# One set of transposes for the samples' x, rows by sequence, and state products on quarters of the array

## The chip, the cores and the metric

The kernel runs on one NeuronCore of a Trainium2 chip. Its engines are TensorE (matrix products; PE in the profile, its weight loads PEld), VectorE (DVE), ScalarE (ACT), GpSimd (POOL) and SyncE (SP), which here only issues transfers. Each engine works through its own list of instructions in order; semaphores make it wait for others. The metric is the device time of one execution in microseconds; the number given for a kernel is the median of its runs.

## What is computed

One step of a decoder layer with two branches, for one prompt of 256 tokens and 8 samples of 8 tokens each (320 tokens in all, D = 2048). The change lies in the second branch, a state-space scan with 32 heads of 64 in 4 groups, state size 128:

```
x = x + RMSNorm( W_out [ chunkMLP(h) || SSD(h) ] )        h = RMSNorm(x)
x = x + RMSNorm( ConvFFN(RMSNorm(x)) )

# SSD, per sequence and head:
h_t = exp(dt_t a) h_{t-1} + dt_t x_t B_t^T        y_t = h_t C_t
# so the state after a sample's 8 tokens is
#   exp(sum of dt a) * state + sum over its tokens of (decay to the end * dt * x_t) B_t^T
```

Each of the 8 samples brings a state of its own (per group 128 x 512: state size by 8 heads of 64), which is read from memory, used, updated and written back.

## The kernel before, in words

**Layout.** Activations stand transposed, 128 features on the partitions and 320 tokens along the row: 256 of the prompt, then 64 of the samples. Products with the big weights run in split float32: each operand is a rounded part (hi) and a remainder (lo), and `accumulate` (lines 151 to 155) makes three products hi*hi, lo*hi, hi*lo of 128 x 128 weights by 320 columns. These are the "ordinary products" of the text. A "slab" is 512 KB of weights: SyncE loads it (`slab`, line 118), ScalarE rounds it (whi, line 124), VectorE subtracts (wlo, line 125); each of raw, hi and lo has three buffers, and a slab feeds some 24 ordinary products.

**Order of the work.** The order of the instructions on every engine is fixed when the program is built, by a planner: it takes instructions by priority, which is their order in the program unless a block is marked as more urgent, and reckons with durations of its own for when an operand will be there. Small work runs in the background: generators (`steps`, `layer_norm`, `gate_mix`, `ssd`, `norm`) are advanced by one step with every `tick` (line 165), one or more ticks behind each slab, so that their instructions stand between ordinary products. The stage of the four `ssd` groups runs from about 430 to 755 us of the trace, beside the last input projections and the products with W_out; its last state update stands at 827 us.

**Time steps (`steps`, 467 to 552).** dt, its softplus, and the sums of dt a are made for five blocks of token rows: two of the prompt, one of the samples, and two in which 32 sample tokens stand fourfold on the 128 partitions (line 473). The decays to the end of a sample come from a mask `later_s`, made by GpSimd in two parts (line 544), each followed by a small TensorE product (line 546) into dec_ps. L773 and L774 are GpSimd copies of the next stage that wait for the same memory as dacsT (the transfer at line 531) to come free.

**B by tokens (775 to 786).** B is transposed by TensorE (`by_token`, line 393; tile bt_ps) for the prompt's two blocks and for the samples' two halves of four samples, the latter copied fourfold first (`fourfold`, line 397). Of the four quarters of partitions two keep the rounded part and two the remainder: bsp.

**One group (`ssd`, 799).** `x_of_samples(i)`, called for each half i = 0, 1, copies x fourfold (x4, line 397), transposes it (four products xt_ps, line 393), multiplies by dt times the decay (xq, line 824), rounds (xsp, line 841), subtracts (line 842), and puts the samples' part of xdt beside it (two products of line 824). The group's states are then taken in four pairs i = 0..3, one of each half of the samples:

- `with_c(i)` (yo_ps, line 887): C times the old states, on TensorE at four column positions of 32.
- `picked(i)` (bm, line 892): ScalarE copies bsp with every row outside the samples of this pair multiplied by zero (bsel).
- `shrunk(i)` (line 898): GpSimd multiplies the old states by their decay.
- `grown(i)` (up_ps, line 904): for either half one TensorE product bm x xsp over all 128 rows, which thus adds the three products hi*hi, hi*lo, lo*hi and a fourth, lo*lo; VectorE adds it to the state (line 906).
- `store_state(i)` (line 911): ScalarE's queue writes the two states back; the fourth pair's are loaded into the memory of the first (lines 805 to 810, six buffers).

The steps are spaced by `yield`: x_of_samples(0); begin(0); a step in which x_of_samples(1) stands; begin(1) and end(0); an empty step; begin(2) and end(1), and so on (lines 932 to 948). `begin` is with_c, picked and shrunk; `end` is grown and store_state. In the last group end(3) is put off behind the last product with W_out (lines 1017 and 1088).

Behind the state updates come the decays within a chunk (`decays`, 956 to 973: ScalarE exponentials cs and cpx, fed by the transfer at line 816) and the products for y (`products`, line 983: y_ps, TensorE at two column positions of 64).

## Time and profile before

| | |
|---|---|
| median of 3 runs | 1779.02 us (1778.82 to 1779.88) |
| profiled execution | 1781.37 us, of which the traced span is 1779.7 us |
| granted TensorE clock, mean over the span | 0.999 |
| VectorE busy | 1168.0 us |
| ScalarE busy | 819.5 us |
| GpSimd busy | 273.5 us |
| moved by transfers | 289.91 MB, 163 GB/s on average |

The profile is that of one execution. A row of a timeline gives start, duration, engine, line and operation, out<-in, partitions x elements and type, and how many such instructions were merged (x8); in brackets the idle time ahead of it and what ended it. For a TensorE product the name of the moving operand comes first, then that of the weights, and "128*32" says rows x columns of the weights. Products are pipelined, so the distance from one start to the next tells more than the duration. The chain is the path of work that ended last, followed back from the end; its rows give start, time on the chain, engine, tile and line. A waits row gives who waited for whom: total us, how many times, the longest.

### The profile page before, as it was taken

To read this page: it belongs to the slowest core of one execution; us is meant where nothing else is said; L and a number is where in the kernel's file an instruction comes from. 1 tells how busy PE (TensorE), PEld (TensorE's weight loads), DVE (VectorE), ACT (ScalarE), POOL (GpSimd) and SP (SyncE) were. 2 spreads that over 40 slices of the span, in tenths; PEclk is the share of its full clock that TensorE was granted. 3 is DMA by queue.
4 is the path that set the end of the run, shared out by engine and by line. 5 is a ranking of instruction groups with operands and counts; after the bars stand their busy time and mean duration, and the time that the engine had idled before them with its cause. 6 is when DMAs were issued, how large, how long until landed. Compare 5 with 4: busy or idle time off the path is not lost.

```text
span 1779.7 us, 30655 instructions
## 1 busy us (share of the span) xinstructions
PE 1770.5 (99%) x11933; PEld 1715.7 (96%) x11933; DVE 1168.0 (66%) x1999; ACT 819.5 (46%) x1195; POOL 273.5 (15%) x602
## 2 busy tenths in 40 slices
PE   9999999999999999999999999999999999999998
PEld 7789999999999998999999999999999999999998
DVE  7549764656977768677865464756656575656575
ACT  5434555334564547445545333343434343433445
POOL 1202200000331313103121011110102020101004
PEclk9999999999999999999999999999999999999999
DMA  7546645456665665554554545545545545454543
GB/s 260 163 148 177 189 128 154 153 153 188 216 190 190 181 207 168 168 171 145 180 156 146 157 149 151 155 148 152 157 144 156 150 150 155 150 150 155 147 154 107
DMA packets 214417, 289.91 MB, mean 163 GB/s; under 512 B 16384, under 2 KB 143744, under 8 KB 214080
## 3 DMA queue, kind: packets, MB, share of 16 engines
q1 hardware_dynamic: 202544, 268.74, 49.6%
q10 hardware_dynamic: 10016, 14.16, 2.2%
q0 software_dynamic: 1712, 5.05, 1.0%
q8 instruction: 94, 1.54, 0.4%
q14 instruction: 51, 0.42, 0.1%
HBM read 273.08 MB, written 14.82 MB: 162 GB/s over the span
## 4 chain that ended last, share of the span: by engine, by line
PE 97%; DVE 1%; ACT 0%; DMA 0%; issue 0%; POOL 0%; POOLq 0%; ACTq 0%; DVEq 0%
PE ps L153 19%; PE ps L155 19%; PE ps L154 19%; PE pd L153 10%; PE pd L155 10%; PE pd L154 10%; PE ps_v L144 7%; PE y_ps L983 1%; PE up_ps L904 0%; PE yo_ps L887 0%; PE sg L731 0%; PE xt_ps L393 0%; DMA cs<-dacs_d 0%; PE x1p L1278 0%; PE tsum L296 0%
## 5 line engine op out<-in xcount | busy, mean ns | idle before, releaser
L125 DVE TENSOR_TENSOR wlo<-wraw,whi 128x1024 fp32r<-128x1024 f32 (+1 forms) x476 | 582.5, 1224 | 432.4 <-ACT whi L124 430.1
L124 ACT CAST whi<-wraw 128x1024 fp32r<-128x1024 f32 (+1 forms) x475 | 494.8, 1042 | 729.9 <-PE ps L154 392.1
L153 PE MATMUL ps<-h_hi,whi 128*128 128x320 f32 x2268 | 704.0, 311 | 0.0
L154 PE MATMUL ps<-h_lo,whi 128*128 128x320 f32 x2268 | 702.7, 310 | 0.0
L155 PE MATMUL ps<-h_hi,wlo 128*128 128x320 f32 x2268 | 702.2, 310 | 0.0
L153 PEld LDWEIGHTS ps<-h_hi,whi 128*128 128x128 f32 x2268 | 426.2, 188 | 2.6 <-issue 1.6
L154 PEld LDWEIGHTS ps<-h_lo,whi 128*128 128x128 f32 x2268 | 426.3, 188 | 0.7
L155 PEld LDWEIGHTS ps<-h_hi,wlo 128*128 128x128 f32 x2268 | 426.2, 188 | 0.0
L155 PE MATMUL pd<-fhi,wlo 128*128 128x320 f32 x704 | 218.2, 310 | 0.0
L153 PE MATMUL pd<-fhi,whi 128*128 128x320 f32 x704 | 218.2, 310 | 0.0
L154 PE MATMUL pd<-flo,whi 128*128 128x320 f32 x704 | 218.2, 310 | 0.0
L153 PE MATMUL pd<-ohi,whi 128*128 128x320 f32 x448 | 139.4, 311 | 0.0
L155 PE MATMUL pd<-ohi,wlo 128*128 128x320 f32 x448 | 138.7, 310 | 0.0
L154 PE MATMUL pd<-olo,whi 128*128 128x320 f32 x448 | 138.7, 310 | 0.0
L153 PEld LDWEIGHTS pd<-fhi,whi 128*128 128x128 f32 x704 | 132.1, 188 | 0.0
L154 PEld LDWEIGHTS pd<-flo,whi 128*128 128x128 f32 x704 | 132.1, 188 | 0.0
L155 PEld LDWEIGHTS pd<-fhi,wlo 128*128 128x128 f32 x704 | 132.1, 188 | 0.0
L1180 POOL COPY ptf<-pad 128x2 f32<-128x2 f32 x88 | 21.0, 239 | 603.7 <-DVE pad L1168 603.0
L249 DVE TENSOR_TENSOR acc_ffn<-acc_ffn,pd 128x320 f32<-128x320 f32 (+1 forms) x161 | 77.5, 482 | 37.8 <-PE pd L155 36.5
L153 PEld LDWEIGHTS pd<-ohi,whi 128*128 128x128 f32 x448 | 84.1, 188 | 1.4 <-issue 1.0
L154 PEld LDWEIGHTS pd<-olo,whi 128*128 128x128 f32 x448 | 84.1, 188 | 0.3
L155 PEld LDWEIGHTS pd<-ohi,wlo 128*128 128x128 f32 x448 | 84.1, 188 | 0.1
(328 smaller groups left out, 1867.9 us busy)
## 6 DMA issues: line engine op xcount, KB each, us to landing
wraw<-in_ffn_w_up SPq DMA_DIRECT2D x176, 512.0 KB, 3.7
wraw<-in_w_in SPq DMA_DIRECT2D x140, 512.0 KB, 3.8
wraw<-in_ffn_w_down SPq DMA_DIRECT2D x88, 512.0 KB, 3.4
wraw<-in_w_out SPq DMA_DIRECT2D x64, 512.0 KB, 3.4
st<-in_state_ssm SPq DMA_DIRECT2D x32, 256.0 KB, 3.9
out_ssm_state_sample<-st ACTq DMA_DIRECT2D x30, 256.0 KB, 3.4
cs<-dacs_d SPq DMA_DIRECT2D x16, 320.0 KB, 4.7
xr<-in_xT SPq DMA_DIRECT2D x4, 640.0 KB, 4.0
```

The costliest lines, as they stand in the source:

```text
L124: rounded[:] = [act.copy(hi, raw).ins]
L125: dve.tensor_tensor(out=lo, in0=raw, in1=hi.bitcast(F32), op=ALU.subtract)
L144: made = pe.matmul(out, xi, w[g][wi], start=first and begins, stop=last and ends)
L153: pe.matmul(ps, whi, xhi, start=first, stop=False)
L154: pe.matmul(ps, whi, xlo, start=False, stop=False)
L155: return pe.matmul(ps, wlo, xhi, start=False, stop=last).ins
L249: added_last[:] = [dve.tensor_tensor(out=acc[:, nb, ts], in0=acc[:, nb, ts], in1=ps[:, ts], op=ALU.add).ins]
L983: pe.matmul(ps[64 * i:64 * i + 64, cols], w(hl), x(hl, m, cpx), tile_position=(0, 64 * i), **flags)
L1180: pool.tensor_copy(ptf[:, k, :], pad[:, 256:258])
```

## The change

- x and B of the samples are transposed once, 64 tokens on 64 partitions, not twice on four copies of 32 tokens. The fourfold copies, the second `x_of_samples` and the masked copies of B (`picked`, bsel) go.
- The rounded part and the remainder are made on these 64 partitions, and then moved by transfers on ScalarE's queue (`by_sequence`) into rows ordered by sequence: partition 4t + c holds part c of the t-th token of a half, so that the 32 rows of one sequence (8 tokens, four parts) are one quarter of the partitions. Eight transfers of 32 rows x 512 elements (64 KB) for B, and eight for x in every group.
- `grown` multiplies 32 rows only, at the row position of the quarter of its sequence (`tile_position=(q, 0)`). The two products of a pair come from different quarters (`of_half`), go to two PSUM tiles and are issued one behind the other, ahead of both additions; the pairs are now samples i of the first half and (i + 1) % 4 of the second.
- `steps` works on three blocks of token rows instead of five: three dt products, one mask `later_s` of 64 x 64, made one step earlier (ahead of csT_ps), and one product with it.

The steps between begin and end, all other loads, stores and products, and the last group's postponed end(3) keep their places. The diff:

```diff
-            for i in range(2):
-                pool.tensor_copy(dtf[:, (3 + i) * P:(4 + i) * P].rearrange("p (q t) -> p q t", q=4),
-                                 dtf[:, NP + 32 * i:NP + 32 * i + 32].unsqueeze(1).to_broadcast([P, 4, 32]))
             yield
             ps = misc("dt_ps")
-            for c in range(5):
+            for c in range(3):
                 pe.matmul(ps[:, NH * c:NH * c + NH], dtf[:, P * c:P * c + P], sums[:, 0], start=True, stop=True)
...
+            later_s = tp.tile([P, NT], F32, tag="pv", name="later_s", bufs=4)[:NS, :NS]
+            pool.tensor_tensor(out=later_s, in0=later[:NS, :NS], in1=bd, op=ALU.mult)
             ps = misc("csT_ps")
             for c in range(2):
                 pe.matmul(ps[:NH, P * c:P * c + P], da[:, c], upper, start=True, stop=True)
...
             pe.matmul(ps[:, 2 * NH:3 * NH], ones, da[:, 1], start=True, stop=True)
-            later_s = tp.tile([P, NT], F32, tag="pv", name="later_s", bufs=4)[:NS, :2 * P].rearrange("p (r q t) -> p r q t", r=2, q=4)
-            for r in range(2):
-                rs = slice(32 * r, 32 * r + 32)
-                pool.tensor_tensor(out=later_s[:, r], in0=later[:NS, rs].unsqueeze(1).to_broadcast([NS, 4, 32]),
-                                   in1=bd[:, rs].unsqueeze(1).to_broadcast([NS, 4, 32]), op=ALU.mult)
-                pe.matmul(ps[:, (3 + r) * NH:(4 + r) * NH], later_s[:, r].rearrange("p q t -> p (q t)"), da[:NS, 2],
-                          start=True, stop=True)
-            act.activation(dec.rearrange("p c h -> p (c h)"), ps[:, :H5], AF.Exp)
-            dve.tensor_tensor(out=dt[:, 3:5], in0=dt[:, 3:5], in1=dec[:, 3:5], op=ALU.mult)
+            pe.matmul(ps[:NS, 3 * NH:4 * NH], later_s, da[:NS, 2], start=True, stop=True)
+            act.activation(dec[:, :3].rearrange("p c h -> p (c h)"), ps[:, :3 * NH], AF.Exp)
+            act.activation(dec[:NS, 3], ps[:NS, 3 * NH:4 * NH], AF.Exp)
+            dve.tensor_tensor(out=dt[:NS, 3], in0=dt[:NS, 2], in1=dec[:NS, 3], op=ALU.mult)
...
             pool.tensor_copy(cb[NS:, NT:], ident[NS:, NS:])
-            for c in range(4):
+            def by_sequence(out, which, parts):
+                rows = out.rearrange("(t c) i n -> t c i n", c=4)
+                for i in range(2):
+                    for c, w in enumerate(which):
+                        act.dma_start(rows[:, c, i].bitcast(F32), parts[w].bitcast(F32)[32 * i:32 * i + 32])
+            for c in range(3):
                 ps = misc("bt_ps")
-                b4 = bT if c < 2 else fourfold(sd.tile([P, 4, P], F32, tag="xde", name="b4", bufs=2), bT, c - 2)
+                n = NS if c == 2 else P
                 for g in range(4):
-                    by_token(ps[:, P * g:P * g + P], b4[:, g], c if c < 2 else 0)
+                    pe.transpose(ps[:n, P * g:P * g + P], bT[:, g, P * c:P * c + n], ident)
                 if c < 2:
                     act.copy(btok[:, c, :], ps)
                 else:
-                    b = bsp[:, c - 2]
-                    act.copy(b, ps)
-                    for rs in (slice(32, 64), slice(96, P)):
-                        dve.tensor_tensor(out=b[rs], in0=ps[rs], in1=b[rs].bitcast(F32), op=ALU.subtract)
+                    parts = [sd.tile([NS, 512], F32R, tag=t, name="part", bufs=n) for t, n in (("bm", 1), ("xde", 2))]
+                    act.copy(parts[0], ps[:NS])
+                    dve.tensor_tensor(out=parts[1], in0=ps[:NS], in1=parts[0].bitcast(F32), op=ALU.subtract)
+                    by_sequence(bsp, (0, 1, 0, 1), parts)
...
+                def of_half(i, h):
+                    return (i + h) % 4
                 def load_state(i):
                     st = [sd.tile([P, 512], F32, tag="st", name="st", bufs=6) for _ in range(2)]
                     for h in range(2):
-                        sp.dma_start(st[h], state_ssm[4 * h + i, g])
+                        sp.dma_start(st[h], state_ssm[4 * h + of_half(i, h), g])
...
-                def x_of_samples(i):
+                def x_of_samples():
                     ps = misc("xt_ps")
-                    x4 = fourfold(sd.tile([P, 4, P], F32, tag="xde", name="x4", bufs=2), xs, i)
                     for j in range(4):
-                        by_token(ps[:, P * j:P * j + P], x4[:, j], 0)
+                        pe.transpose(ps[:NS, P * j:P * j + P], xs[:, j, NP:NT], ident)
                     xq = sd.tile([P, 512], F32, tag="xde", name="xq", bufs=2)
-                    times(xq, ps, 3 + i)
-                    act.copy(xsp[:, i], xq)
-                    dve.tensor_tensor(out=xsp[64:, i], in0=xq[64:], in1=xsp[64:, i].bitcast(F32), op=ALU.subtract)
+                    at = slice(0, NS)
+                    times(xq[at], ps[at], 3, at)
                     for r in range(2):
-                        at = slice(64 - 64 * r + 32 * i, 96 - 64 * r + 32 * i)
-                        times(xdt[at, 2, 256 * r:256 * r + 256], ps[at, 256 * r:256 * r + 256], 2, at, slice(4 * r, 4 * r + 4))
+                        times(xdt[64 - 64 * r:P - 64 * r, 2, 256 * r:256 * r + 256], ps[at, 256 * r:256 * r + 256], 2, at,
+                              slice(4 * r, 4 * r + 4))
+                    parts = sd.tile([NS, 512], F32R, tag="bm", name="high", bufs=1), xq[at].bitcast(F32R)
+                    act.copy(parts[0], xq[at])
+                    dve.tensor_tensor(out=parts[1], in0=xq[at], in1=parts[0].bitcast(F32), op=ALU.subtract)
+                    by_sequence(xsp, (0, 0, 1, 1), parts)
...
-                x_of_samples(0)
+                x_of_samples()
                 yield
...
-                            pe.matmul(ps_yo[row:row + 32, :256], cms[:, 4 * h + i, :], st[h][:, 256 * r:256 * r + 256],
+                            pe.matmul(ps_yo[row:row + 32, :256], cms[:, 4 * h + of_half(i, h), :], st[h][:, 256 * r:256 * r + 256],
                                       start=i == 0, stop=i == 3, tile_position=(0, row))
-                def picked(i):
-                    bm = sd.tile([P, 2, P], F32R, tag="bm", name="bm", bufs=2)
-                    act.activation(bm, bsp[:, :, bs].bitcast(F32), AF.Copy, scale=bsel[:, i:i + 1])
-                    return bm
                 def shrunk(i, st):
                     with first():
                         for h in range(2):
                             pool.tensor_tensor(out=by_head(st[h]), in0=by_head(st[h]),
-                                               in1=tote[:, h0:h0 + 8, 4 * h + i:4 * h + i + 1].to_broadcast([P, 8, 64]), op=ALU.mult)
-                def grown(st, bm):
+                                               in1=tote[:, h0:h0 + 8, 4 * h + of_half(i, h):4 * h + of_half(i, h) + 1].to_broadcast([P, 8, 64]), op=ALU.mult)
+                def grown(i):
+                    ps = [misc("up_ps") for _ in range(2)]
                     for h in range(2):
-                        ps = misc("up_ps")
-                        made = pe.matmul(ps, bm[:, h], xsp[:, h], start=True, stop=True)
+                        q = 32 * of_half(i, h)
+                        made = pe.matmul(ps[h], bsp[q:q + 32, h, bs], xsp[q:q + 32, h], start=True, stop=True, tile_position=(q, 0))
+                    for h in range(2):
                         with first():
-                            dve.tensor_tensor(out=st[h], in0=st[h], in1=ps, op=ALU.add)
+                            dve.tensor_tensor(out=sts[i][h], in0=sts[i][h], in1=ps[h], op=ALU.add)
                     return made.ins
                 def store_state(i, st, by=act):
                     for h in range(2):
-                        by.dma_start(o_ssm_s[4 * h + i, g], st[h])
+                        by.dma_start(o_ssm_s[4 * h + of_half(i, h), g], st[h])
...
-                bms = {}
                 def begin(i):
                     with_c(i, sts[i])
-                    bms[i] = picked(i)
                     shrunk(i, sts[i])
                 def end(i, by=act):
-                    made = grown(sts[i], bms.pop(i))
+                    made = grown(i)
                     store_state(i, sts[i], by)
                     return made
...
-                    if i == 0:
-                        x_of_samples(1)
                     yield
                 begin(3)
                 yo_to_xdt()
```

26 lines of the change are left out of this document (11 added, 15 removed).

## The prediction

> **What bounds the kernel now.** I read the page first, then TensorE's waits, then the time where those waits stand. From the page:
>
> ```profile
> span 1779.7 us, 30655 instructions
> ...
> PE 1770.5 (99%) x11933; PEld 1715.7 (96%) x11933; DVE 1168.0 (66%) x1999; ACT 819.5 (46%) x1195; POOL 273.5 (15%) x602
> ...
> PE 97%; DVE 1%; ACT 0%; DMA 0%; issue 0%; POOL 0%; POOLq 0%; ACTq 0%; DVEq 0%
> ```
>
> TensorE's waits (total us, how many, longest):
>
> ```profile
> PE dec_ps L546 <- POOL later_s L544: 1.0, 2, 0.7
> PE up_ps L904 <- DVE xsp L842: 0.8, 2, 0.6
> ```
>
> TensorE sets the end: 99% busy and 97% of the chain. VectorE, ScalarE and the queues count only where TensorE waits for them, and two of its few waits stand on lines that the change rewrites. So the sum has three parts: TensorE instructions taken out, these waits, and new waits.
>
> **The wait for later_s (L544).** TensorE's timeline:
>
> ```profile
> 244.29 0.39 PE L153 MATMUL ps<-h_hi,whi 128*128 128x320 f32 x1
> 245.02 0.41 PE L546 MATMUL dec_ps<-sp_e,later_s 64*128 64x32 f32 x2 [0.34 <-POOL later_s L544]
> ...
> 247.23 0.47 PE L153 MATMUL ps<-h_hi,whi 128*128 128x320 f32 x1
> ```
>
> Two windows behind it (the number before the last two is the granted clock):
>
> ```profile
> 247.00:250.40 3.40, 3.40 (x14) 3.40 (x15) 0.22 (x1) 0.20 (x1) 0.00 (x0) 0.53 0.55 154
> 250.40:253.80 3.40, 3.40 (x25) 3.40 (x24) 0.97 (x1) 1.36 (x2) 0.00 (x0) 1.00 0.00 0
> ```
>
> GpSimd's timeline:
>
> ```profile
> 243.81 0.33 POOL L773 COPY cb_cms<-ident 64x64 f32<-64x64 f32 x1 [25.68 <-PE ps L154]
> ```
>
> From 244.29 to 247.23 TensorE starts three ordinary products and the two of later_s. Ordinary products start 0.146 us apart (24 of them from 468.61 to 472.12, in a fence below), so 2.94 - 0.44 = 2.5 us are lost. Then the granted clock is 0.53 for 3.40 us: 3.40 x 0.47 = 1.6 us more, of which some 0.2 is counted twice. Loss: 3.9 us. The change has one mask product on 64x64 instead of two on 64x128, one step of the background work earlier, and GpSimd runs it ahead of L773 and L774 instead of behind them. Its inputs are masks from the kernel's start, and GpSimd sat idle for 25.68 us ahead of L773, so it should be done before TensorE asks. One small product stays, 0.41 us by its row, and 0.1 behind it. I take **-3.4 us**; bounds 0 (still late) and -3.9.
>
> **Transposes and small products taken out.** Rows of the chain:
>
> ```profile
> 442.52 0.44 PE xt_ps L393 x4
> ...
> 452.79 0.67 PE up_ps L904 x2
> ...
> 488.07 1.69 PE y_ps L983 x32
> ...
> 507.68 0.45 PE cb_ps L856 x4
> ```
>
> Four transposes take 0.44 us. The second x_of_samples goes in each of four groups, and B's transposes go from 16 to 12: 5 x 0.44 = **-2.2 us**, all on the chain. The transposes that stay for the samples have 64 columns of weights and stream 128 columns as now, so I leave them at their price. Two of the five dt products (L479) go too; by the row of the later_s product, 0.41 us, between 0 and -0.8: I take **-0.4 us**.
>
> **States by quarters (L904).** A pair is now two products over 128 rows; then it is two over 32 rows each, at different row positions. TensorE's timeline:
>
> ```profile
> 467.22 0.31 PE L155 MATMUL pd<-ohi,wlo 128*128 128x320 f32 x1
> 467.46 0.64 PE L887 MATMUL yo_ps<-st,cb_cms 128*32 128x256 f32 x8
> 468.03 0.74 PE L904 MATMUL up_ps<-xsp,bm 128*128 128x512 f32 x2
> 468.61 0.31 PE L153 MATMUL pd<-ohi,whi 128*128 128x320 f32 x1
> ...
> 472.12 0.62 PE L904 MATMUL up_ps<-xsp,bm 128*128 128x512 f32 x2
> 472.58 0.31 PE L153 MATMUL pd<-ohi,whi 128*128 128x320 f32 x1
> ```
>
> Start to start, a pair takes 0.46 us among ordinary products (472.12 to 472.58), 0.23 for each, and 0.58 behind yo_ps, which works at column positions. So coming back from positions to the whole array costs about 0.1; going there costs as much (467.22 to 467.46 is 0.24, not 0.146). No row shows two row positions side by side. Column positions do overlap: y_ps is 12 products of 128 columns and 4 of 64, which one after another at cb_ps's price (0.45 for two of 128) would take 3.2 us, and takes 1.69. Bounds for a pair among ordinary products: -0.23 (full overlap, positions free) and +0.3 (no overlap, 0.1 on each side, 0.1 for weights that nothing hides). The nearest row is yo_ps: 0.1 on entry, 0.57, 0.1 on leaving, for products that stream for 0.45 (256 columns at cb_ps's price): 0.32 over the streaming. With it, a pair among ordinary products costs 0.23 + 0.32 = 0.55 instead of 0.46. Behind yo_ps, where a return is paid already, it costs some 0.05 less than now. Ten of the 16 pairs begin behind yo_ps: 6 x 0.09 - 10 x 0.05 = 0; since the second quarter's weights may come unhidden I take **+0.3 us**. Bounds -3.7 and +4.8.
>
> The Trainium skill speaks on both sides. "TensorE: Matmul & The Clock Gate", section "Measured speedup vs the span model", gives a pack of tiles the time of one product and about 4 ns more for each further tile; by it the pairs would save 3.7 us, and y_ps's overlap agrees. "TensorEngine Tiling (Array Packing)", section "Key Properties", says that a change of tiling mode drains the engine; the 0.24 us ahead of yo_ps agrees, and by it next to nothing is left.
>
> **Transfers in place of copies.** The present wait for xsp is one for the second x_of_samples, which goes: **-0.8 us**. In its stead one x_of_samples feeds eight transfers of 64 KB on ScalarE's queue, two of each four behind VectorE's subtraction. TensorE's timeline in the second group, then VectorE's:
>
> ```profile
> 518.07 0.64 PE L887 MATMUL yo_ps<-st,cb_cms 128*32 128x256 f32 x8
> ...
> 522.01 0.47 PE L904 MATMUL up_ps<-xsp,bm 128*128 128x512 f32 x1 [0.24 <-DVE xsp L842]
> ```
>
> ```profile
> 513.16 0.68 DVE L824 TENSOR_TENSOR xq<-xt_ps,dt 128x512 f32<-128x512 f32 x1
> 513.76 1.21 DVE L125 TENSOR_TENSOR wlo<-wraw,whi 128x1024 fp32r<-128x1024 f32 x1
> 515.00 1.45 DVE L842 TENSOR_TENSOR xsp<-xq,xsp 64x512 fp32r<-64x512 f32 x1
> 516.48 0.85 DVE L824 TENSOR_TENSOR xdt<-xt_ps,dt 32x256 f32<-32x256 f32 x2
> ```
>
> The store's line L911 (ns, least/median/most), and issues by size with us to landing:
>
> ```profile
> L911 ACTq DMA_DIRECT2D out_ssm_state_sample<-st x30: 338/338/784, 455.1 to 712.7; - x30
> ```
>
> ```profile
> out_y<-acc_ffn SPq DMA_DIRECT2D x5, 160.0 KB, 1.9
> ...
> out_ffn_conv_sample<-stg ACTq DMA_DIRECT2D x22, 32.0 KB, 1.5
> ```
>
> The new chain in the second group: VectorE as now up to 515.00, then the xdt products (0.85) and the subtraction (up to 1.45): 517.3. Six more issues at 0.34: 519.3. Landing, 1.5 to 1.9: **521**. The order of the program wants the pair behind yo_ps, at 518.2 (518.07 + 0.57 - 0.44 for the transposes gone). So the operand comes 2 to 3 us after its place, here and in the fourth group, whose steps are spaced alike. In the first group the place lies 10 us behind the transposes (442.52 to 452.79), in the third nearly as far, and the chain just fits. But TensorE's order isn't the program's: the planner that fixes it put the second product of this pair at 522.01, behind a slab's worth of ordinary products, and its reckoning was short by only 0.24 us here and 0.6 at the other place, over a chain of about 4 us (518.07 to 522.01). Over a chain twice as long I take 1.0 us in each of two groups: **+2.0 us**. Bounds: 0, and four groups at 3 us with a slow clock behind each. Queued behind a waiting pair are all ordinary products, so such a wait counts in full.
>
> The issues also hold ScalarE: ahead of the third stands a wait for VectorE, and behind it the next whi copy, for which wlo and then TensorE wait. From the page:
>
> ```profile
> L124 ACT CAST whi<-wraw 128x1024 fp32r<-128x1024 f32 (+1 forms) x475 | 494.8, 1042 | 729.9 <-PE ps L154 392.1
> ```
>
> Most of the idle time ahead of whi is a wait for TensorE to free a buffer, so ScalarE is early; and 8 x 0.34 = 2.7 us of issues replace the four bm, two x4 copies and one of the two xsp copies of a group. I cost this at nothing; without that cover it is up to 1 us a group. The eight transfers of B have until 452.79 and cost nothing, or one wait of rival 1's price. VectorE loses half of its x_of_samples work, hidden either way. Taking two PSUM banks at once costs nothing, since pairs already use two in a row.
>
> **Sum.** -3.4 - 2.2 - 0.4 + 0.3 - 0.8 + 2.0 = **-4.5 us**. The profiled execution took 1781.37 us, 1.67 of it around its span, so it would take 1776.9. The median of the runs before is 2.35 lower, 1779.02; the same microseconds off it give **1774.5 us**.
>
> **Rivals.**
> 1. *The transfers are late in two groups and the clock falls.* The planner reckons them short: waits of 2.0 us, and a slow stretch behind each as at 247, 1.6 us. 2 x 3.6 = 7.2 instead of 2.0: **1779.7**. For it: 521 against 518.2. Against it: no slow stretch followed the waits of 0.24 and 0.6 us. The Trainium skill ("TensorE: Matmul & The Clock Gate", section "What's actually happening") asks for an idle window of about 3.4 us, by which 2 us would leave the clock alone; here some 2 us of lost time in pieces, 244.29 to 247.23, was enough.
> 2. *Slower: the transfers are late in all four groups*, because their issues stand in ScalarE's order between the exponentials of the decays. Price 2.5 + 1.6 = 4.1 a group, 16.4: **1788.9**. All else saves 6.5, so the kernel is slower by over 0.2% (3.6 us) once the waits pass 10.1, or 2.5 a group. Against it: the 10 us of the first group.
> 3. *Quarters run one after the other.* 16 x 0.23 = 3.7 on the forecast: **1778.2**. Against it: y_ps.
> 4. *Quarters overlap and positions are free*, the rule on the span: -3.7 instead of +0.3: **1770.5**. Against it: 0.1 us on both sides of yo_ps.
> 5. *The mask product is still late* (the change doesn't do what it says): +3.4, **1777.9**. Against it: GpSimd's 25 idle us.
>
> **How the numbers follow.** Forecast 0.46 (own range 1771.5 to 1775.4), rival 1 0.20, rival 2 0.18, rivals 3 and 4 0.06 each, rival 5 0.04. About 0.2% is what a measurement of this kernel can tell from no change. Faster: forecast and rival 4, 0.52. Same: rivals 1, 3 and 5, 0.30. Slower: rival 2, 0.18. The range 1770.0 to 1783.0 holds all but most of rival 2.
>
> **What would show it.** Right: no wait of TensorE for later_s and no slow stretch near 247; one xt_ps group of four for the samples of each group; pairs of 0.5 to 0.55 us; waits of up_ps for transfers of about 1 us in the second and fourth groups. Wrong: an up_ps row that waits 2 us or more with a granted clock near 0.5 behind it (rivals 1, 2), pairs of 0.8 (3) or 0.25 (4), later_s still among TensorE's waits (5).

## The result: 0.28% slower, and where the time stands

Before: 1779.61 us, the median of 9 runs. After: **1784.91 us** (9 runs, 1783.2 to 1786.41). The ratio is 1.0028, 95% interval 1.0020 to 1.0036: slower by some 5.3 us, where 4.5 less were forecast. From the page of the changed kernel (profiled execution 1785.27 us):

```profile
span 1783.4 us, 30585 instructions
...
PE 1771.7 (99%) x11907; PEld 1710.7 (96%) x11907; DVE 1154.8 (65%) x1980; ACT 810.4 (45%) x1169; POOL 275.9 (15%) x595
...
PE 95%; DMA 3%; DVE 1%; ACT 1%; issue 0%; ACTq 0%; SPq 0%; DVEq 0%
```

There are fewer instructions on TensorE (11907, it was 11933), VectorE and ScalarE, and yet the span is longer. The chain tells why: TensorE's share went from 97% to 95%, and 3% is now transfers, which were at 0%. TensorE's waits (total us, how many, longest):

```profile
PE yo_ps L890 <- DMA st<-in_state_ssm: 3.2, 1, 3.2
PE early L70 <- DVE ones L66: 1.1, 1, 1.1
PE up_ps L904 <- DMA xsp<-xq: 1.0, 2, 0.6
PE ps L148 <- DVE acc_mix L244: 0.7, 2, 0.5
```

The waits for later_s and for xsp by VectorE are gone. The waits for transfers of x make 1.0 us, and a wait that no step of the prediction had, 3.2 us for the load of a state, is the largest. Seven of the nine runs have a mean clock of 0.999 or 0.998; the two at 1.000 took 1783.20 and 1784.05 us, so the change is slower without a slow stretch too.

**The mask.** TensorE's timeline:

```profile
243.34 0.53 PE L533 MATMUL dec_ps<-sp_e,later 128*128 128x32 f32 x4
243.71 0.39 PE L534 MATMUL dec_ps<-sp_e,ones 128*128 128x32 f32 x2
244.02 0.30 PE L535 MATMUL dec_ps<-sp_e,later_s 64*64 64x32 f32 x2
244.25 0.42 PE L148 MATMUL ps<-h_hi,whi 128*128 128x320 f32 x1
```

No wait in brackets, and the next ordinary product starts 0.23 us behind the mask product.

**The pairs.** TensorE's timeline in the first group, around a single product and around a pair:

```profile
452.72 0.49 PE L904 MATMUL up_ps<-xsp,bsp 32*128 32x512 f32 x1
453.14 0.41 PE L150 MATMUL ps<-h_hi,wlo 128*128 128x320 f32 x1
```

```profile
468.09 0.31 PE L150 MATMUL pd<-ohi,wlo 128*128 128x320 f32 x1
468.32 0.50 PE L904 MATMUL up_ps<-xsp,bsp 32*128 32x512 f32 x2
468.75 0.42 PE L148 MATMUL pd<-ohi,whi 128*128 128x320 f32 x1
469.01 0.31 PE L149 MATMUL pd<-olo,whi 128*128 128x320 f32 x1
```

From start to start, a single quarter holds TensorE for 0.42 us, a pair for 0.43: two quarters overlap completely. Around the pair, 0.23 and 0.26 stand where ordinary products need 0.146.

**The transfers.** ScalarE's timeline in the last group, then the durations of the issues (ns, least/median/most; first and last start):

```profile
696.48 0.62 ACT L846 CAST high<-xq 64x512 fp32r<-64x512 f32 x1
...
697.13 1.14 ACTq L769 DMA_DIRECT2D xsp<-high  x2
698.30 0.62 ACTq L769 DMA_DIRECT2D xsp<-xq  x1
699.59 1.05 ACT L119 CAST whi<-wraw 128x1024 fp32r<-128x1024 f32 x1 [2.12 <-PE pd L149]
699.59 0.48 ACTq L769 DMA_DIRECT2D xsp<-xq  x1
700.11 1.25 ACTq L769 DMA_DIRECT2D xsp<-high  x2
701.40 1.25 ACTq L769 DMA_DIRECT2D xsp<-xq  x2
```

```profile
L769 ACTq DMA_DIRECT2D xsp<-high x16: 477/605/653, 444.0 to 700.7; - x16
```

One issue takes 0.605 us, not the 0.34 of a store, and the fourth stands 0.67 us behind the end of the third, since a whi copy ahead of it in ScalarE's list waits for TensorE. The second half's transfers are issued from 700.11 to 702.65; the last issue ends 5.5 us behind the start of the first. The second product of the first pair stands behind a further slab in the planner's order, and in the last group this runs on:

```profile
703.47 0.49 PE L904 MATMUL up_ps<-xsp,bsp 32*128 32x512 f32 x1
704.53 0.64 PE L890 MATMUL yo_ps<-st,cb_cms 128*32 128x256 f32 x8
707.35 0.73 PE L904 MATMUL up_ps<-xsp,bsp 32*128 32x512 f32 x3
709.67 0.50 PE L904 MATMUL up_ps<-xsp,bsp 32*128 32x512 f32 x2
713.82 0.62 PE L890 MATMUL yo_ps<-st,cb_cms 128*32 128x256 f32 x2
717.60 0.63 PE L890 MATMUL yo_ps<-st,cb_cms 128*32 128x256 f32 x6 [3.16 <-DMA st<-in_state_ssm]
```

The chain (start, time on it) shows what lies between 707 and 717:

```profile
707.42 0.44 PE up_ps L904
707.96 0.70 DVE st L907
708.68 4.13 DMA out_ssm_state_sample<-st
712.89 4.67 DMA st<-in_state_ssm
717.60 0.63 PE yo_ps L890 x6
```

The late product makes the sum late, the sum the store, and the fourth pair's state is loaded into the very memory that this store reads. A product of 0.4 us with no wait of its own is followed by a wait of 3.16 us at a place 10 us further on. Two windows there (TensorE busy, granted clock, DMA share, GB/s):

```profile
714.00:717.60 3.60, 0.44 (x3) 1.00 0.94 296
717.60:721.60 4.00, 4.00 (x20) 0.60 0.05 15
```

Behind the wait the clock stands at 0.60 for 4.0 us: 1.6 us more. The Trainium skill ("TensorE: Matmul & The Clock Gate", section "What's actually happening") has the clock fall after an idle window of about 3.4 us; here 3.16 us was enough.

The direct wait of 0.64 us in the first group has a further cause, in ScalarE's timeline:

```profile
443.35 0.62 ACT L846 CAST high<-xq 64x512 fp32r<-64x512 f32 x1 [3.54 <-DMA bsp<-part]
```

The rounded part of x (high) goes into the same buffer (tag bm) as the rounded part of B, and its copy waits 3.54 us until B's transfers have read it. Only then can x's transfers start, at 444.00.

The same TensorE instructions in four profiles (start in us; the second profile of the kernel before and the kernel without transfers belong to the experiments below):

| | before | before, again | after | without x's transfers |
|---|---|---|---|---|
| first s_ps of group 1 | 442.95 | 440.58 | 438.28 | 438.05 |
| fin_ps behind group 1 | 505.79 | 503.42 | 504.31 | 500.94 |
| tsum behind group 3's states | 640.49 | 638.71 | 639.91 | 635.71 |
| fourth pair's yo_ps, group 4 | 714.95 | 713.17 | 713.82 | 709.39 |
| tsum behind group 4's states | 744.99 | 743.21 | 749.14 | 739.63 |

The change leads the second profile of before by 2.3 us when the groups begin, is 1.2 us behind it when the third group's states are done, and loses 5.3 us between the last two rows.

### The profile page after: what moved, and what is told of

Read it like the earlier page. It is cut to its first block, busy times and chain, and to the rows that moved or that the text cites. A ratio compares the mean times of both kernels' runs of the same rounds, so it can differ in the third digit from the quotient of the medians.

```text
span 1783.4 us, 30585 instructions
## 1 busy us (share of the span) xinstructions
PE 1771.7 (99%) x11907; PEld 1710.7 (96%) x11907; DVE 1154.8 (65%) x1980; ACT 810.4 (45%) x1169; POOL 275.9 (15%) x595
## 4 chain that ended last, share of the span: by engine, by line
PE 95%; DMA 3%; DVE 1%; ACT 1%; issue 0%; ACTq 0%; SPq 0%; DVEq 0%
PE ps L148 18%; PE ps L149 18%; PE ps L150 18%; PE pd L148 10%; PE pd L150 10%; PE pd L149 10%; PE ps_v L139 7%; PE y_ps L979 1%; DMA bsp<-part 1%; DMA out_ssm_state_sample<-st 1%; PE sg L720 0%; PE yo_ps L890 0%; DMA cs<-dacs_d 0%; PE up_ps L904 0%; DMA wraw<-in_w_in 0%
```

## The experiments

Each expectation stands as it was on record. The kernel before was run beside each on the same chip; its medians lay between 1779.28 and 1780.34 us, and each ratio is to these. The planner makes the order anew for each kernel, so neighbouring products move too; I read nothing from differences under 1 us between medians.

### The early mask alone (kernel before)

```diff
+            later_s = ...            # both parts, ahead of csT_ps
             ps = misc("csT_ps")
```

> The kernel before with one edit: GpSimd makes both parts of later_s one step earlier. The theory of the prediction's first term (the late mask costs 2.5 us of waits and 1.6 us of a lower clock near 247): 3.4 to 3.9 us faster than before, no row of TensorE waiting for later_s, granted clock 1.00 from 247 to 250. Rival (the wait only moves to the next late operand, or the clock falls anyway): less than 1 us. It says nothing on the states.

Measured: 1779.71 us, ratio 0.9996 (0.9988 to 1.0005): no gain. And yet its profile stands 3.05 us ahead of the prediction's profile at the same instruction near 258 us. In the groups TensorE then waits 2.1 us for xsp, where the prediction's profile has 0.8.

### The kernel before, profiled again

> The kernel before, once more, for a second profile. The run with the early mask had a profile 3 us ahead at 250 us, but no better median. Theory (the slow clock behind the mask's wait is not there in most executions; 24 of 27 runs of the kernel before had a mean clock of 1.000 to three digits, the profiled one 0.999): dec_ps still waits about 1 us for later_s, no slow stretch at 247 us, span 1777 to 1778. Rival (the stretch is always there and the early mask's gain is lost later): the clock near 247 us is about 0.6 again, span 1779 to 1780.

Measured: 1779.6 us, span 1777.9. Among its waits, then two of its windows (TensorE busy, clock, DMA share, GB/s):

```profile
PE dec_ps L546 <- POOL later_s L544: 0.2, 1, 0.2
```

```profile
247.00:250.40 3.40, 3.40 (x25) 1.00 0.57 154
250.40:253.80 3.40, 3.40 (x25) 1.00 0.23 47
```

Where the first profile showed a clock of 0.53 there is none of it, and the wait is 0.2 us, not 1.0. Of the 27 runs of the kernel before beside the first four experiments, 24 have a mean clock of 1.000, which a stretch that loses 1.6 us of 1780 would lower to 0.999. So **most executions lack the slow stretch**. This second profile is 2.4 us ahead of the first at 258 us; there the early mask is worth 3.05 - 2.4 = 0.7 us. The first experiment's flat median agrees, with the longer waits for xsp (2.1 us for 0.8 in this profile too) as the likely place where the 0.7 went.

### The mask late again (changed kernel)

```diff
-            later_s = ...            # ahead of csT_ps
+            later_s = ...            # ahead of its product
```

> The changed kernel with the mask made where it was before, just ahead of its product. By the theory that the mask's place is worth 3.4 to 3.9 us by itself: that much slower than the changed kernel, about 1788.5. By the rival (the one smaller mask is quick enough wherever it is made): within 1 us of it.

Measured: 1787.89 us, ratio 1.0038 (1.0025 to 1.0050), 3 us over the changed kernel in only 5 runs. Its profile, the fastest of the five at 1783.52, waits 0.4 us for later_s, and shows no slow stretch at 247 us or elsewhere ahead of the end. The other four runs have a mean clock of 0.997 or 0.998, so most of their 3 to 5 us over this one goes with a slow clock, at places that no trace shows. So I put no size on it.

### The rounded part's transfers first

```diff
-                for i in range(2):
-                    for c, w in enumerate(which):
+                for c, w in sorted(enumerate(which), key=lambda p: p[1]):
+                    for i in range(2):
```

> The changed kernel with the eight transfers issued in another order: all four of the rounded part first, then the four that wait for VectorE's subtraction. Theory A (the first pair's second update comes late, so its state is stored late, the fourth pair is loaded late into its memory, and TensorE waits 3.2 us for that load in the last group, with 1.6 us of a lower clock behind): the last transfers are issued about 1.2 us earlier, the wait shrinks by about that or goes; 1 to 5 us faster than the changed kernel. Theory B (the loss lies in the quarter products and their changes of position): within 1 us of it.

Measured: 1784.3 us, ratio 1.0024 (1.0015 to 1.0032). That is 0.6 us under the changed kernel, where theory A wanted 1 to 5 and theory B less than 1; the full rows below speak against B's cause. TensorE waits for no transfer of x any more, but 3.7 us for state loads, 2.6 of them in the last group. The direct waits are not the price.

### No store of the first pair in the last group

```diff
-                    store_state(i, sts[i], by)
+                    if (g, i) != (3, 0):
+                        store_state(i, sts[i], by)
```

> The changed kernel without the store of the first pair of states of the last group; it leaves out writing these two outputs. Theory A (the fourth pair's load waits for that store): TensorE's wait for the load near 714 and the lower clock behind it go, 4 to 5 us faster than the changed kernel, about 1780.3. Theory B (quarter products): within 1 us of the changed kernel.

Measured: 1781.96 us, ratio 1.0015 (1.0006 to 1.0024), 3.0 us under the changed kernel. The two windows of the last group:

```profile
714.00:717.60 3.60, 3.60 (x29) 1.00 0.73 226
717.60:721.60 4.00, 4.00 (x29) 1.00 0.48 135
```

The hole is gone, and in this profile the slow clock with it. The chain from store to load is shown as a cause, but for 3 us only: eight of the eleven runs still have a mean clock under 1.000, so a slow stretch stands somewhere in most of them.

### Products over all rows, and no transfers: four cells

Full rows:

```diff
-    pe.matmul(ps[h], bsp[q:q + 32, h, bs], xsp[q:q + 32, h], ..., tile_position=(q, 0))
+    pe.matmul(ps[h], bsp[:, h, bs], xsp[:, h], ...)
```

No transfers:

```diff
-    by_sequence(xsp, (0, 0, 1, 1), parts)
+    act.copy(xsp[at, i], xq[at])                     # for both i
+    dve.tensor_tensor(out=xsp[NS:, i], in0=xq[at], in1=xsp[at, i], op=ALU.subtract)
```

> The changed kernel, but each state product runs over all 128 rows and without a row position, as in the kernel before. It leaves out the separation of the sequences: each product sums four of them. Transfers, their order and everything else stay. Theory (two causes: 3 us for the quarter products, 4 to 5 us for the chain transfers - late first update - late store - late load in the last group): the sum from start to next start over the 32 state products falls from 10.6 us to about 7.5 us, the wait of yo_ps for the load in the last group stays (2 to 3 us), and the median falls by about 3 us, to 1781.5 to 1782.5. Rival (the position changes cost nothing that the neighbours wouldn't fill, all of the loss is the chain): no change, 1784 to 1785.

> The changed kernel with the quarter products, but x's parts are written straight to their tile by ScalarE copies and VectorE subtractions, without the 32 transfers for x. It leaves out the ordering of x's rows by sequence, so the products multiply rows that don't belong together. Theory (chain of the last group): no wait of up_ps for a transfer, the first pair of every group runs as one pair, its store starts about 4 us earlier in the last group, no wait of yo_ps over 0.5 us; the median falls by 4 to 5 us, to 1780 to 1781. Rival (the loss sits in the products' positions): still 1783 to 1785.

> Both at once: products over all 128 rows and x's parts written without transfers. It leaves out both the separation and the ordering of the sequences. What stays of the change is one set of transposes for x, two dt products less, the early mask and no masked copies. Theory: the two costs add up, so 7 to 8 us less than the changed kernel, 1776.5 to 1778, that is 2 to 3 us under the kernel before: the transposes' 2.2 us and the dt products' 0.4 us, with little left of the mask's 3.4 us, since the run with the early mask alone showed none of it in the median. Rival (mask term real, but eaten by the transfers): 1774 to 1776. Rival (transposes' gain is not there either): 1779 to 1780.

Measured medians in us:

| | transfers for x | none |
|---|---|---|
| quarters | 1784.91 | 1775.13 |
| full rows | 1785.02 | 1775.17 |

Ratios to before: full rows 1.0030 (1.0021 to 1.0040), no transfers 0.9974 (0.9965 to 0.9983), neither 0.9972 (0.9962 to 0.9982). The expected 3 us for the quarters show in neither column. Without the transfers no pair is split, so the single products that I had added up are not there, and 16 of the 19 runs stand at a mean clock of 1.000: 1775.13 and 1775.17. With them the clocks differ (five of ten runs with full rows have 0.998 or less, one of nine with quarters), so something may be hidden there. The quarters cost nothing that shows, and **the transfers for x cost 9.8 us**, nearly twice the loss. B's eight transfers stay in all four cells; no run takes them alone away. The last group without transfers (the table above has its starts):

```profile
700.73 0.50 PE L903 MATMUL up_ps<-xsp,bsp 32*128 32x512 f32 x2
705.25 0.50 PE L903 MATMUL up_ps<-xsp,bsp 32*128 32x512 f32 x2
709.39 0.64 PE L889 MATMUL yo_ps<-st,cb_cms 128*32 128x256 f32 x8
```

No pair is split, and the fourth pair's yo_ps waits for nothing. By the table the 9.5 us between the two spans lie thus: 0.2 ahead of the first s_ps, 3.1 in group 1, 0.8 more up to 640, 0.2 up to the fourth pair's yo_ps, 5.1 behind it, most of which is the wait of 3.16 and the 1.6 of the slow clock. TensorE's starts tell where the 3.1 in group 1 lie: the wait at 448.31 some 0.7, the split pair 0.6, y_ps at 484.42, which is interrupted by an ordinary product, 0.9, and two waits for acc_mix (VectorE's sum of the W_out products) near 497, with the restarts behind them, 1.0. (The kernel without transfers has 1.3 us of a wait of its own at the head of group 2.)

### Issued, but unread

```diff
+    rows = sd.tile([P, 2, 256], F32, tag="bm", name="unread", ...).rearrange("(t c) i n -> t c i n", c=4)
+    act.dma_start(rows[:, c, i], xq[32 * i:32 * i + 32, :256])       # for all c and i: eight in each group
```

> The kernel without transfers for x (x's parts written straight to their tile, rows not by sequence: it leaves out their ordering), and in addition eight transfers per group on ScalarE's queue, of half the width, into a tile that nobody reads. So the issuing is there and nothing waits for what lands. Theory I (ScalarE's time): 1779 to 1783, at least half of the 9.8 us comes back. Theory L (late operands): 1775 to 1776.5, like the kernel without transfers.

Measured: 1775.47 us, ratio 0.9978 (0.9969 to 0.9988). Its issues:

```profile
L851 ACTq DMA_DIRECT2D unread<-xq x32: 477/605/975, 443.3 to 694.7; - x32
```

The same 0.605 us each, 32 of them, cost nothing: ScalarE's time is free, as costed. What is left is the late operand, and the memory that the transfers hold while they read. (They moved half the bytes, so full traffic is not quite tried.)

### Other queues, for x's transfers

```diff
-    act.dma_start(rows[:, c, i]...)
+    sp.dma_start(rows[:, c, i]...)            # and, in another run, pool.dma_start
```

> The changed kernel with the whole computation; the 32 transfers for x are issued on SyncE's queue, B's eight stay on ScalarE's. The four runs before it showed that the transfers for x are worth 9.8 us (1775.1 us without them) and the quarter products nothing. Open is which side of them costs. Theory I (ScalarE is held by issuing them, some 10 us in every group, so that the exponentials and the rounding of slabs behind them are late): the median falls to 1777 to 1780, if the slabs on SyncE's queue bear 5 us of issue per group. Theory L (xsp is complete too late for the first pair, from whatever queue): 1783 to 1786, with the wait for the fourth pair's load still in the last group.

> The changed kernel with the whole computation; the 32 transfers for x are issued on GpSimd's queue, where only the shrinking of the states and small products stand. Theory I: 1777 to 1780, if GpSimd takes no more than about 1 us for each. Theory L: the order of the first updates stays late; 1783 to 1787, later still if an issue on GpSimd is slower than the 0.6 us on ScalarE, since the shrinking of the states then stands behind the transfers.

Measured: 1783.19 us on SyncE's queue (ratio 1.0030, 1.0017 to 1.0042), 1799.06 on GpSimd's (1.0113, 1.0100 to 1.0126). SyncE's has the time of theory L without its sign: no wait for a load stands in the last group; s_ps waits 1.5 us for x0d (x times the decay, made by GpSimd in one of the two buffers that xq shares), and up_ps 1.0 for xsp. TensorE's waits on GpSimd's:

```profile
PE up_ps L904 <- DMA xsp<-xq: 9.5, 5, 3.9
PE yo_ps L890 <- DMA st<-in_state_ssm: 3.7, 2, 3.0
```

This is what rival 2 of the prediction would have looked like: direct waits in every group, 9.5 us of them, with five slow stretches (mean clock 0.995).

### An earlier start

```diff
-                x_of_samples()            # behind cms
+                x_of_samples()            # at the head of the group
                 for c in range(2):
```

> The changed kernel with the whole computation; only x_of_samples stands at the head of the group's first step, ahead of the prompt's transposes, so that its transfers are issued some 5 us earlier. Theory (the transfers are too late for the first pair, and all the rest of the chain follows from that): no wait of up_ps for a transfer, first pair not split, the last group's store 3 to 4 us earlier, the wait of yo_ps for the load gone or under 1 us; the median falls by 3 to 4.5 us, to 1780.5 to 1782. Rival (the transfers cost by their mere traffic and issue time, wherever they stand): 1784 to 1785. Against the kernel before it stays 1 to 2 us slower by the theory, since the quarter products keep their 3 us.

> The changed kernel with the whole computation; x_of_samples stands at the head of the group in groups 2 to 4 only and keeps its place in group 1; the remainder of B waits for its transfers in s1's memory instead of one of the two xde buffers. The move in all groups had put TensorE 8 us behind the run without transfers in group 1, where x0d waited for an xde buffer that B's transfers still read, and only 2.3 us more in groups 2 to 4. Theory (late operand in groups 2 to 4 mends itself by the earlier start; group 1 alone keeps its 1.5 us): 1777.5 to 1779.5, no wait of yo_ps for a load over 0.5 us. Rival (the earlier start takes xde or VectorE away from the group before in every group): 1781 to 1785.

> The changed kernel with the whole computation; x_of_samples at the head in all four groups, and both parts of B in memory that nobody asks for at that time (a cs buffer and s1), so that in group 1 neither x0d nor the rounding of x waits for B's transfers. Theory (every late operand mended, only the first pair of group 1 still close, since x's transfers stand behind B's eight on the queue): 1776 to 1779, s_ps waits under 0.5 us. Rival (group 1 loses again, the xde buffer of xq itself is what x0d waits for): a wait of s_ps of 2 to 3 us and 1780 to 1783.

Measured: 1786.46 us at the head of every group (ratio 1.0038, 1.0025 to 1.0050), 1781.85 in groups 2 to 4 only, with B's remainder in other memory (1.0013, 1.0004 to 1.0022), 1782.98 in all groups with both of B's parts in other memory (1.0021, 1.0012 to 1.0031). In none does yo_ps wait for a load, but each has new waits; the three in turn:

```profile
PE s_ps L879 <- POOL xde L830: 3.3, 1, 3.3
PE s_ps L879 <- DMA xsp<-high: 1.4, 1, 1.4
```

```profile
PE s_ps L882 <- DMA xsp<-high: 2.6, 1, 2.6
```

```profile
PE up_ps L905 <- DMA xsp<-high: 1.4, 1, 1.4
PE s_ps L880 <- POOL xde L831: 1.0, 1, 1.0
```

The transfers hold xq's and high's memory longer than copies did, and what is now behind them, x0d and s_ps, waits. Behind the waits of 3.3, 2.6 and 1.4 us the three profiles show 3.4 us at a clock of 0.51, which adds 1.7 us each time. Half of the theory holds: an earlier start takes 3 us off at best.

### A seventh state buffer

```diff
-  name="st", bufs=6      name="cs", bufs=3
+  name="st", bufs=7      name="cs", bufs=2
```

> The changed kernel with the whole computation, with a seventh state buffer (one of the two loads of the fourth pair no longer waits for the first pair's store) and two cs buffers instead of three to make room. Theory (the chain store - load costs 3 us of the median in the last group, the rest of the transfers' price lies before): if it is the load into the second half's memory that is late, taking away one load leaves the other unless the seventh buffer serves it; 1782 to 1784, wait of yo_ps for the load halved or gone. Rival (two cs buffers hold up the decays): 1785 or more, with longer waits of y_ps for cs.

Measured: 1790.6 us, ratio 1.0062 (1.0050 to 1.0075). The wait for state loads is down to 0.5 us, but y_ps waits 4.9 us for cs: the rival. On the chain it says little, since the missing cs buffer costs more than the added state buffer can save.

### The order of the rows without transfers

Two TensorE products with a matrix of zeros and ones instead (`order`, 128 x 128, one for each half); then the same with fewer waits; then the layout of before, filled by engines:

```diff
-    act.dma_start(rows[:, c, i]..., parts[w]...)
+    pe.matmul(ps[i], order[:, k, i], out[:, 0], start=True, stop=True)
+    act.copy(out[:, i], ps[i])
```

> The changed kernel with the whole computation and no transfers for x or B: the rounded part and the remainder are written to the two halves of partitions of their tile, and two TensorE products with a matrix of zeros and ones put the rows of either half by sequence; ScalarE copies them back. This adds two products of 512 columns to each group and two for B (10 by 0.23 us, the spacing of full-row products of 512 columns: 2.3 us) and leaves the path from x to the products on engines, about 3 us long, where the transfers took 5 to 7 us. Theory (the price of the change is the lateness of the operand and nothing else, and the kernel without transfers at 1775.1 us is what the rest of it brings): 1775.1 + 2.3 = 1777.4, range 1776.5 to 1778.5, no wait of yo_ps for a load and pairs of up_ps not split; that is 2 us under the kernel before. Rival (the first pair stays late by the two copies, and the fourth pair's load with it): 1780 to 1783.

> The run before it (rows put in order by TensorE products with a matrix of zeros and ones, the whole computation, no transfers for x or B) with two waits taken away that its trace shows: the matrices are made by 8 GpSimd copies instead of 16, B's first (TensorE waited 1.2 us for them), and x's two ordering products stand one place later, behind the first pair's products with C instead of straight behind the subtraction (TensorE waited 1.9 us for VectorE there). Theory (nothing but waits at those places separates it from the 1777.4 us that the sum gives): 1776.5 to 1778.5, no wait of rows_ps over 0.3 us, first pairs unsplit. Rival (the later products make the first pair late, so the price moves to the state updates or to the fourth pair's load): 1779.5 to 1782, with waits of up_ps for xsp.

```diff
+    act.copy(out[:32, i], x[32 * i:32 * i + 32])               # and a second copy
+    dve.tensor_tensor(out=out[lo, i], in0=x[...], in1=out[:32, i], op=ALU.subtract)
+    pool.tensor_copy(out[lo + 32, i], out[lo, i])
```

> The whole computation with one set of transposes for the samples' x and B, as in the changed kernel, but in the layout of the kernel before: the four quarters of rows are written by engines (four ScalarE copies, two VectorE subtractions and two GpSimd copies of 32 rows for each group's x), the masked copies of B and the products over 128 rows stay as before, and there are no transfers for x or B. So TensorE does what it did in the run without transfers and with full rows (1775.2 us), and the operand is on engines alone, about 3 us behind xq. Theory (the gain is the transposes, the dt products and the waits that went; the loss is the lateness of a transferred operand): 1776 to 1778, 2 to 3 us under the kernel before. Rival (anything that makes the first pair's operand later than in the kernel before, by whatever means, gives the gain back, as in the two runs with ordering products): 1779.5 to 1782.

Measured: 1780.03, 1780.65 and 1780.10 us, ratios 1.0002 (0.9993 to 1.0011), 1.0007 (0.9997 to 1.0016) and 1.0003 (0.9994 to 1.0012). The theory misses in all three, and the times are the rivals': 5 us better than the change, no better than before. Waits of the second and of the third:

```profile
PE rows_ps L778 <- DVE xsp L856: 2.1, 2, 1.6
```

```profile
PE up_ps L916 <- POOL xsp L778: 3.4, 4, 1.5
```

Each has its direct waits where the operand is late, in the planner's fixed order; moving the two products one place later in the program did not take their wait away. The third adds nothing to TensorE, which speaks for a late operand rather than for TensorE's added work; its 3.4 us of waits make up most of the 4.9 us that it stands above the kernel with neither transfers nor quarters (1775.17), and what makes the rest stays open. No version here beats the kernel before with the whole computation.

## Why the prediction was wrong, by its steps

- **Transfers in place of copies: +2.0 forecast, 9.8 measured.** This step failed, and turned a gain into a loss. Its direct part was half of the forecast: 1.0 us of waits, in groups 1 and 2 rather than 2 and 4. In group 1 the chain was said to just fit, and B's transfers to cost nothing; but those hold the buffer that x's rounded part needs (3.54 us). Above all, the step asked only which instruction waits for xsp. It gave the planner credit for moving a late product behind a slab, and did not follow what hangs on that product: sum, store, the load into the same memory, the fourth pair's yo_ps. That chain is in the trace of before, with little to spare (in its second profile the last of these loads is issued at 708.8 and lands 2.7 us later, some 1.5 us ahead of its reader). There, the late product of the first pair and the fourth pair's yo_ps:

```profile
703.89 0.47 PE L904 MATMUL up_ps<-xsp,bm 128*128 128x512 f32 x1 [0.57 <-DVE xsp L842]
...
713.17 0.64 PE L887 MATMUL yo_ps<-st,cb_cms 128*32 128x256 f32 x8
```

  From the one to the other are 9.28 us without a wait. In the changed kernel the chain from 707.42 to 717.60 takes 10.18, from a start that is 3.5 us later. It is worth 3.0 us by the run without the store. The rest shows in the table, above all the 3.1 us in group 1, most of them not a wait for xsp but what comes behind it: a split pair, y_ps in pieces, waits for acc_mix. That the transfers cause these is shown, since the run without them has no split pair, no interrupted y_ps and no such wait in its list; by which of their effects, the late operand or the held buffer, is not.
- **The price of an issue: 0.34 forecast, 0.605 measured.** Six issues more are 3.6 us, not 2.0; the place of the second group's operand moves from 521 to about 523. Costing ScalarE's time at nothing was right (the unread transfers).
- **The mask: -3.4 forecast, about -0.7 measured.** The wait was read rightly, but from one execution, whose slow clock 24 of 27 others don't have; a second profile has 0.2 us of the wait's 1.0 as well. "The same microseconds off the median" carried it over.
- **Transposes -2.2, dt products -0.4, the wait for xsp -0.8, quarters +0.3.** They and the mask's 0.7 make -3.8; without transfers the kernel is 4.7 us under the runs of before beside it (1775.13 for 1779.81). As a sum these terms held, with 0.9 us to spare. The first two can be read singly: from each such product to TensorE's next start, added up over the second profile of before and over the change, xt_ps takes 6.7 and 5.0 us, bt_ps 1.7 and 1.1, dt_ps 1.0 and 0.6. For the quarters the full overlap, 0.43 for 0.42, agrees with the Trainium skill ("TensorE: Matmul & The Clock Gate", section "Measured speedup vs the span model"): a further tile costs next to nothing. What it would save goes on both sides of the pair, 0.23 and 0.26 for 0.146, as the prediction took from yo_ps; by these rows a pair among ordinary products costs 0.43 + 0.09 + 0.11 = 0.63 us for 0.46, so 0.17 more, not 0.09.
- **The rivals.** Rival 1 had the fall of the clock right, 1.6 us, but at the wrong wait. Rival 2 had the right side and the wrong mechanism: the waits for xsp make 1.0 us, not 10. With the mask at 0.7 and the transfers at 9.8 the sum would have been -0.7 - 2.2 - 0.4 + 0.3 - 0.8 + 9.8 = +6.0; 5.3 was measured.

## What to carry to other kernels

When an operand gets later, follow the memory as well as the engines: list what the delayed result's store frees, and who loads into it; a chain that just fits before can be a wait afterwards, far from the line that was changed. A transfer that replaced an on-chip copy was paid for in lateness and held memory here, not in issue time: 32 issues cost nothing when nobody read what they moved. And before a stall with a slow clock is entered into a sum, look at the mean clocks of the other runs: a stretch that most of them lack is no gain to be had.

## What was not expected of the hardware

- A transfer of 32 rows between partitions took 0.605 us to issue on ScalarE's queue, a store of 128 rows 0.34; halving its bytes changed nothing (0.605 again).
- A product of 32 rows and 512 columns at a row position held TensorE for 0.42 us, alone or in a pair, where one over 128 rows takes 0.23 in a row of its kind. A third product, which shares its quarter with one of the pair, adds 0.23 (the three at 707.35 take 0.66 up to the next start). So about 0.2 us goes with the change of position, once for the whole set.
- A wait of 3.16 us was followed by 4.0 us at a clock of 0.60, in a profile whose mean clock is 0.999. With the earlier start in all groups and B's parts in other memory, a wait of 1.4 us was followed by 3.4 us at 0.51; on SyncE's queue one of 1.5 us was followed by no slow stretch.
